# Expert weights in 1 MB loads with 8 KB rows instead of 512 KB loads with 4 KB rows

## The chip, the cores and the metric

The kernel runs on one core of a Trainium2 chip. The metric is the device time of one execution in microseconds (us); the median of three runs counts. TensorE (PE) multiplies matrices; its weight loads (PEld) overlap its products. VectorE (DVE), ScalarE (ACT) and GpSimd (POOL) work element by element, and SyncE (SP) does little more than issue DMA transfers. A core has 16 DMA engines, which share all transfers. "Share" of DMA is the mean busy share of these 16, and can pass 1 a little, since packets overlap in the records.

## The reference

Two transformer-like blocks run one after the other on 256 tokens of width 1024, all in fp32. The first mixes a convolution with a window attention and then sends each token to 2 of 32 experts. The second mixes a long convolution with an attention over the tokens and 256 context rows, and then runs a PEER layer: for each token and each of 8 heads, 16 of 16,384 small experts are looked up by product keys. Cut to what the change touches:

```python
def run_block(args):                       # MoE: 32 experts, D = 1024, F = 512
    tok, wt, e = args
    xb = xt[tok]
    hmid = jax.nn.silu(xb @ w_gate[e]) * (xb @ w_up[e])
    return (hmid @ w_down[e]) * wt[:, None]

def chunk(xc):                             # PEER: 8 heads, 2 x 128 keys
    q = (xc @ wq).reshape(PEER_CHUNK, PEER_HEADS, 2, half)
    s1 = jnp.einsum('chd,hnd->chn', q[:, :, 0], keys1)
    s2 = jnp.einsum('chd,hnd->chn', q[:, :, 1], keys2)
    ...                                    # top 16 of 16 x 16 sums: experts eidx, gates g
    a = jnp.einsum('chkd,cd->chk', u_tab[eidx], xc)
    return jnp.einsum('chk,chkd->cd', gelu(a) * g, v_tab[eidx])
```

An expert's gate and up matrices are 1024 x 512, its down matrix 512 x 1024: 2 MB each, 6 MB in all, and 192 MB for 32 experts.

## The kernel before, in words

All weights are streamed from HBM once, and nearly all go through one helper, `wload` (L67 to L88). It takes the next buffer of a ring (`self.wpools`, walked by the counter `wi`) and has SP issue one transfer of 512 KB into it: 128 partitions, 4 KB in each. A buffer is a pool's tile, so its transfer waits until the last reader of what stood in it is done. SP issues its transfers in the order of its own instruction list: one that waits for a buffer holds up those behind it.

The ring changes with the stage. `wA` has 4 buffers throughout. The first mix (0 to 204 us) has `wA` and 7 buffers of `wB`; the expert stage (204 to 694 us) has 4 `wA`, 7 `wB` and 3 `wC`, 14 buffers or 7 MB, and before them takes 16 places that are free just once (`self.early`: tiles of `l2`, `wE` and the split buffers `hi` and `lo`), so that experts' weights arrive during the first mix. The second mix (694 to 920 us) has 4 `wA` and 3 `wD`; its last part and the query product have `wA` alone; PEER has `wA`, `hi`, `lo` and four parts of a tile named `xm`.

In the expert stage TensorE follows the order in which the program is written (L846 to L893; the order is pinned). For expert e: `expert_up` (L1023, the product in L1031) takes four pairs of a gate and an up load; for each of its 8 slices of 128 rows it runs one gate and one up product side by side in the two halves of the array's columns, 16 products in 8 pairs, each product of 512 columns being listed by the profile in more than one piece. Then `expert_down` (L1050, the product in L1060) of expert e-1 takes four loads of the down matrix, each for two products. Then come a slice of background work of the second block, the transposes and SiLU of expert e (L1042 to L1047), and for every second expert the return of the results to the tokens (`combine`, L1078). Ahead of expert 28 stands a branch on the chip (L924) for experts with more than 64 tokens, which these inputs don't take; 8 loads of expert 28 are issued ahead of it.

In the mixes and in the query product a weight is split for exact fp32 into `hi` (ACT, L97) and `lo` (DVE, L98); its buffer is free when both are done. The query product has 16 columns of `wq`, one load each, and two loads of the keys (`keysT`, L1574), each of which serves 8 columns and holds a `wA` buffer for so long.

Of the kernel before, what the change touches and what calls it, by code (L numbers as in the profile page):

```python
# [44 lines left out]
class K:  # L45
# [20 lines left out]

    def wload(self, src, shape, eng=None):  # L67
        pools = self.wpools
        p, tag = pools[self.wi % len(pools)]
        self.wi += 1  # L70
        if p is None:

            v = tag[:, :math.prod(shape)]
            if len(shape) == 2:
                v = v.rearrange("p (a b) -> p a b", a=shape[0])
            (eng or self.nc.sync).dma_start(v, src)
            return v
        if self.wrap and self.wi == len(pools):
            self.wpools, self.wrap, self.wi = self.wrap, None, 0
        t = self.T(p, [128, 1024], F32, tag)  # L80
        n = 1
        for s in shape:
            n *= s
# [96 lines left out]
    def build(self):  # L180
        tc, nc, A = self.tc, self.nc, self.A
        with ExitStack() as es:
            keep = es.enter_context(tc.tile_pool(name="keep", bufs=1))
            self.keep = keep
            self.wA = es.enter_context(tc.tile_pool(name="wA", bufs=4))
            self.hp = es.enter_context(tc.tile_pool(name="hp", bufs=3))
# [11 lines left out]
            with ExitStack() as e1:  # L198
                self.l1 = l1 = pool(e1, "l1")
                self.l2 = pool(e1, "l2")  # L200
                ew = ExitStack()
                wB = pool(ew, "wB", 7)
                self.wpools = [(self.wA, "wA")] * 4 + [(wB, "wB")] * 7
                self.h = self.T(l1, [128, 2, D], F32, "h")
# [25 lines left out]
                with ExitStack() as e2:  # L230
                    self.me = pool(e2, "me")
                    self.wE = ExitStack()

                    r = self.wi % len(self.wpools)
                    self.wpools = self.wpools[r:] + self.wpools[:r] + [(pool(e2, "wC", 3), "wC")] * 3
                    self.early = [(self.l2, n) for n in ("kv", "kfc", "kfa0", "kfb0", "kfa1", "kfb1")]
                    self.early += [(pool(self.wE, "wE", 4), "wE")] * 4 + [(self.hp, "hi")] * 3 + [(self.hp, "lo")] * 3
# [501 lines left out]
    def moe(self):  # L739
# [103 lines left out]
        def gu(e):  # L843
            return [lambda kq, w=w: w[e][:, 2 * kq:2 * kq + 2, :] for w in (wg, wu)]

        def experts(lo, hi, pre=None, cur=None):  # L846
# [7 lines left out]
            for e in range(lo, hi + 1):  # L854

                if e < hi:
                    if e % 4 == 0 and e > lo:
                        cur = nxt
                    st = self.expert_up(*gu(e), cur[0][:, :, (e % 4) * 64:(e % 4) * 64 + 64], pre if e == lo else None)
                if e > lo:  # L860
                    y = self.expert_down(mid, lambda j: wd[e - 1][:, j, :], (e - 1) % 2, sws[0],
                                         y if e % 2 == 0 else None)
                if e < hi:
                    back(e)
                    mid = self.expert_mid(st)
                    if pend:
                        self.combine(*pend)
                        pend = None
                    if e % 2 == 0:
                        sws.append(self.selw(cur[1], e % 4))  # L870
                    if e % 4 == 2 and e + 2 < 32:
                        nxt = group(e + 2)
                    back(e, True)
                if e > lo and e % 2 == 0:
                    if pend:
                        self.combine(*pend)
                    pend = y, sws.pop(0)
# [22 lines left out]
        pools = self.wpools  # L900
        self.wi = 0
        self.wpools = pools + self.early
# [5 lines left out]
        pools = self.wpools  # L908
        self.wi = 0
# [3 lines left out]
        self.wpools, self.wi = pools, 8  # L913
        self.gf = self.T(self.hp, [128, D], F32, "hi")
# [5 lines left out]
    def overflow(self, many, wg, wu, wd):  # L920
# [3 lines left out]
        with self.tc.If(many > 64):  # L924
# [12 lines left out]
            for j in range(7):  # L937
# [28 lines left out]

                st = self.expert_up(lambda kq: part(wg, 2 * kq, 2), lambda kq: part(wu, 2 * kq, 2), XT)
                m = self.expert_mid(st)
                sw = self.selw(sw, 0, 1)
                y = self.expert_down(m, lambda i: part(wd, i, 1).rearrange("p k f -> p (k f)"), 0, sw)  # L970
                self.combine(y, sw, 1)
# [47 lines left out]

    def up_load(self, g, u, kq):  # L1020
        return [self.wload(f(kq), [2, 512]) for f in (g, u)]

    def expert_up(self, g, u, XT, pre=None):  # L1023
        nc, me = self.nc, self.me
        p = self.ps()
        for kq in range(4):
            w = pre[kq] if pre else self.up_load(g, u, kq)
            for a in range(2):
                k = 2 * kq + a
                for s in range(2):  # L1030
                    nc.tensor.matmul(p[64 * s:64 * s + 64, :], XT[:, k, :], w[s][:, a, :],  # L1031
                                     start=k == 0, stop=k == 7)
        ex = self.T(me, [128, 512], F32, "ex", 2)
        nc.scalar.activation(ex, p, AF.Copy)
        return ex
# [190 lines left out]
    def mix2(self):  # L1226
# [132 lines left out]
        self.m2e.close()  # L1359
        self.wpools = [(self.wA, "wA")]  # L1360
        self.px = self.rpool("px")
# [180 lines left out]
    def peer(self):  # L1542
# [27 lines left out]
        for m in range(16):  # L1570
            if m > 2:
                next(rg, 0)
            if m % 8 == 0:
                kt = self.wload(A["keysT"][:, m * 128:(m + 8) * 128].rearrange("p (m n) -> p m n", m=8), [8, 128])  # L1574
            if m in first:
# [5 lines left out]
            if late:  # L1581
                score(*late)
            late = (m, q, kt[:, m % 8, :])
            if m == 4:
# [6 lines left out]
        w4 = self.T(self.px, [128, 4, 1024], F32, "xm")  # L1591
        self.wpools = [(self.wA, "wA")] * 4 + [(self.hp, "hi")] * 3 + [(self.hp, "lo")] * 3
        self.wpools += [(None, w4[:, i, :]) for i in range(4)]
        self.wi = 0
        gb = ga = self.pace_pe = None
# [559 lines left out]
```

## Time and profile before

| what | us |
|---|---|
| three runs | 1623.05, 1625.93, 1627.79 |
| median | 1625.93 |
| the profiled execution's own time | 1625.43 |
| its span | 1623.6 |

The span lies 1.8 us below the time of its own execution, and that time 0.5 us below the median. TensorE is busy for 94% of the span, DVE for 59%, ACT for 31%. The core moves 536 MB, 426 MB of them on SP's queue (q1). The mean TensorE clock granted is 0.972 of full speed. Stages are cut by the lines that run: first mix to 204, experts to 694, second mix to 920, query product and routing to 1004, PEER's first table to 1305, gathers to 1404, PEER's second table to the end.

In a timeline row the columns are the start and the duration in us, engine, line, operation, output and input tiles, and in brackets the idle time of the engine ahead of it and what ended it; "issue" means that it waited for nothing that the profile shows. In a list of waits, the engine and line that waited stand left of the arrow and what it waited for right of it, then total us, times, and the longest.

### The profile page before, as it was taken

How to read it: one execution, taken by the hardware profiler on the slowest of the kernel's cores; microseconds unless marked ns; L12 is line 12 of the kernel's file. 1: busy time of each engine (PE TensorE's matmuls, PEld its weight loads, DVE VectorE, ACT ScalarE, POOL GpSimd, SP SyncE). 2: the span in 40 equal slices, each digit the busy share in tenths (PEclk: the TensorE clock that was granted, in tenths of full speed). 3: DMA queues.
4: the chain of work that ended last, by engine and by line, in shares of the span. 5: the costliest groups of instructions: out<-in, count | busy, mean ns of one | idle time of the engine just before them, and what ended most of it. 6: DMA issues, size and time to landing. Idle time of an engine off the chain costs nothing. (4 is left out here: it accounts for less than half of the span.)

```text
span 1623.6 us, 25732 instructions
## 1 busy us (share of the span) xinstructions
PE 1527.8 (94%) x9872; PEld 1200.8 (74%) x9872; DVE 960.9 (59%) x2117; ACT 496.0 (31%) x1222; POOL 120.1 (7%) x122
## 2 busy tenths in 40 slices
PE   7999799999999997979999899999999999699996
PEld 6978644543444443358679699999999999699996
DVE  6986622344535432279888899856667656544443
ACT  4444332232222221155344543235444400000001
POOL 0000000000000000000000100311111112111111
PEclk9999899999999998989999999999999999799998
DMA  9548779999999998965657558999999999999992
GB/s 371 182 132 301 273 277 381 381 418 410 418 419 418 419 418 342 417 223 155 210 185 270 185 169 303 376 404 345 366 363 356 357 409 415 416 413 413 414 414 80
DMA packets 135324, 536.53 MB, mean 330 GB/s; under 512 B 16179, under 2 KB 17180, under 8 KB 122780
## 3 DMA queue, kind: packets, MB, share of 16 engines
q1 hardware_dynamic: 117184, 426.07, 69.1%
q0 software_dynamic: 13824, 100.67, 15.5%
q10 hardware_dynamic: 4188, 8.09, 1.4%
q8 instruction: 79, 1.29, 0.3%
q14 instruction: 49, 0.40, 0.1%
HBM read 532.57 MB, written 2.10 MB: 329 GB/s over the span
## 5 line engine op out<-in xcount | busy, mean ns | idle before, releaser
L1793 DVE SCALAR_TENSOR_TENSOR g<-g,xd 128x1024 f32<-128x1024 f32 x96 | 117.5, 1224 | 140.6 <-DMA g<-in_uv_dram,gi 140.6
L1031 PE MATMUL ps<-wB,XT 128*64 128x512 f32 x492 | 133.2, 609 | 4.7 <-PEq L924 4.6
L1765 POOL DMA_INDIRECT g<-in_uv_dram,gi x96 | 98.8, 1029 | 505.6 <-PE ps L1648 121.1
L132 PE MATMUL ps<-xh,hi 128*128 128x256 f32 x416 | 122.9, 296 | 1.6 <-ACT hi L97 1.6
L1067 DVE SCALAR_TENSOR_TENSOR eyl<-ps,slotw,eyh 64x512 fp32r<-64x512 f32 x64 | 47.6, 743 | 119.0 <-ACT eyh L1066 118.7
L138 PE MATMUL ps<-xh,lo 128*128 128x256 f32 x416 | 117.4, 283 | 0.5 <-DVE lo L98 0.5
L137 PE MATMUL ps<-xl,hi 128*128 128x256 f32 x416 | 117.5, 283 | 0.3 <-DVE xl L305 0.3
L1794 ACT ACTIVATE ga<-ga 128x1 f32<-128x1 f32 x96 | 19.4, 202 | 314.9 <-DVE g L1793 314.9
L1031 PEld LDWEIGHTS ps<-wB,XT 128*64 128x64 f32 x492 | 39.6, 139 | 80.5 <-issue 74.0
L97 ACT ACTIVATE hi<-wA 128x1024 fp32r<-128x1024 f32 x63 | 66.6, 1059 | 76.6 <-PE ps L137 28.8
L98 DVE TENSOR_TENSOR lo<-wA,hi 128x1024 fp32r<-128x1024 f32 x63 | 77.7, 1237 | 20.2 <-ACT hi L97 18.2
L1640 PE MATMUL ps<-x,wA 128*128 128x160 f32 x608 | 87.4, 302 | 0.1
L1648 PE MATMUL ps<-B,wA 128*128 128x160 f32 x608 | 85.9, 300 | 0.0
L1640 PEld LDWEIGHTS ps<-x,wA 128*128 128x128 f32 x608 | 84.9, 193 | 0.3 <-issue 0.3
L132 PEld LDWEIGHTS ps<-xh,hi 128*128 128x128 f32 x416 | 79.3, 191 | 7.7 <-issue 4.4
L1080 DVE TENSOR_TENSOR h<-h,ps 128x512 f32<-128x512 f32 x64 | 42.2, 682 | 70.3 <-PE ps L1078 70.3
L1648 PEld LDWEIGHTS ps<-B,wA 128*128 128x128 f32 x608 | 83.5, 190 | 0.0
L137 PEld LDWEIGHTS ps<-xl,hi 128*128 128x128 f32 x416 | 79.4, 191 | 3.9 <-issue 3.1
L1640 PE MATMUL ps<-x,xm 128*128 128x160 f32 x576 | 81.4, 299 | 0.0
L1648 PE MATMUL ps<-B,xm 128*128 128x160 f32 x576 | 81.2, 302 | 0.0
L1779 DVE SCALAR_TENSOR_TENSOR xd<-g,gw,xd 128x1024 f32<-128x1024 f32 x62 | 79.7, 1285 | 2.1
L1648 PEld LDWEIGHTS ps<-B,xm 128*128 128x128 f32 x576 | 80.1, 193 | 0.0
(531 smaller groups left out, 3364.4 us busy)
## 6 DMA issues: line engine op xcount, KB each, us to landing
wB<-in_w_gate_dram SPq DMA_DIRECT2D x70, 512.0 KB
wB<-in_w_down_dram SPq DMA_DIRECT2D x63, 512.0 KB
wB<-in_w_up_dram SPq DMA_DIRECT2D x53, 512.0 KB
wA<-in_ws_dram SPq DMA_DIRECT2D x51, 512.0 KB
wA<-in_ut_dram SPq DMA_DIRECT2D x38, 512.0 KB
wA<-in_v_dram SPq DMA_DIRECT2D x38, 512.0 KB
wA<-in_w_gate_dram SPq DMA_DIRECT2D x36, 512.0 KB
wA<-in_w_up_dram SPq DMA_DIRECT2D x36, 512.0 KB
```

What stands on the lines that cost most here:

```text
L97: ins = self.nc.scalar.activation(hi, w, AF.Copy)
L98: self.last_split = self.nc.vector.tensor_tensor(lo, w, hi.bitcast(F32), op=OP.subtract)
L132: ins = mm(ps, ah, bh, start=first, stop=False)
L137: mm(ps, ah, bl, start=False, stop=False)
L138: mm(ps, al, bh, start=False, stop=last)
L1031: nc.tensor.matmul(p[64 * s:64 * s + 64, :], XT[:, k, :], w[s][:, a, :], start=k == 0, stop=k == 7)
L1067: nc.vector.scalar_tensor_tensor(y[1][r, s, :], p[r, :], w, y[0][r, s, :].bitcast(F32), op0=OP.mult, op1=OP.subtract)
L1640: self.pace_pe = nc.tensor.matmul(p, w[:, k, :], x32[:, k, N0:], start=k == 0, stop=k == 7)
L1648: self.pace_pe = nc.tensor.matmul(acc[k][:, N0:], w[:, k * 128:(k + 1) * 128], B[:, c, :], start=c == 0, stop=c == 127)
L1765: ins = nc.gpsimd.indirect_dma_start(out=buf[i], out_offset=None, in_=A["uv"], in_offset=bass.IndirectOffsetOnAxis(ap=self.gi[:, i // J, i ...
L1779: stt(acc, t, w, acc, op0=OP.mult, op1=OP.add)
L1793: stt(t, t, 1.0, self.gx[s], op0=OP.mult, op1=OP.mult, accum_out=a)
```

## The change

The rings are rebuilt from tiles that hold two loads (8 KB per partition, 1 MB). A pool's entry now says how many halves a tile has. `wload` still loads 512 KB; where the tile has two halves, the next call fills the second half of the same tile, which is a transfer of its own. A new helper, `wload2`, is used by the experts alone: it fills a whole tile with one transfer of 1 MB, a row of 8 KB in each partition. So `up_load` now fetches half a gate and half an up matrix in two transfers where four stood, and `expert_down` half a down matrix. A tile is free when both its halves have been read.

The rings: first mix 2 `wA` and 3 `wB` of 1 MB (10 halves where there were 11); experts 2 + 3 + 2 (7 MB as before); the places for the early loads are the same, four of them now two tiles of 1 MB; second mix 2 `wA` of two halves and 3 `wD` of one; query product 2 `wA` of two halves. The counter is reset where a ring begins. The two loads of `keysT` become one of 1 MB into a buffer of the gather pool (`g`), which is not in use then. The arithmetic is unchanged.

```diff
-    def wload(self, src, shape, eng=None):
+    def pools(self, *groups):
+        self.wpools = [g[:2] + g[3:] for g in groups for _ in range(g[2])]
+        self.wi, self.half = 0, None
+    def wload(self, src, shape, eng=None):
+        n = math.prod(shape)
+        if self.half is None:
+            p, tag, m = self.wnext()
...
+                t = self.T(p, [128, 1024 * m], F32, tag)
+            if m > 1:
+                self.half = t[:, 1024:]
+        else:
+            t, self.half = self.half, None
...
+    def wload2(self, src, shape):
+        if self.half is None and self.wpools[self.wi % len(self.wpools)][2] > 1:
+            p, tag, m = self.wnext()
+            t = self.T(p, [128, 2048], F32, tag).rearrange("p (i a b) -> p i a b", i=2, a=shape[0])
+            self.nc.sync.dma_start(t.rearrange("p i a b -> p (i a) b"), src(0, 2))
+            return [t[:, i] for i in range(2)]
+        return [self.wload(src(i, 1), shape) for i in range(2)]
...
-            self.wA = es.enter_context(tc.tile_pool(name="wA", bufs=4))
+            self.wA = es.enter_context(tc.tile_pool(name="wA", bufs=2))
...
-                wB = pool(ew, "wB", 7)
-                self.wpools = [(self.wA, "wA")] * 4 + [(wB, "wB")] * 7
+                self.pools((self.wA, "wA", 2, 2), (pool(ew, "wB", 3), "wB", 3, 2))
...
-                    self.wpools = self.wpools[r:] + self.wpools[:r] + [(pool(e2, "wC", 3), "wC")] * 3
+                    self.wpools = self.wpools[r:] + self.wpools[:r] + [(pool(e2, "wC", 2), "wC", 2)] * 2
...
-                    self.wpools = [(self.wA, "wA")] * 4 + [(pool(self.m2e, "wD", 3), "wD")] * 3
+                    self.pools((self.wA, "wA", 2, 2), (pool(self.m2e, "wD", 3), "wD", 3, 1))
...
-        pre = [self.up_load(*gu(28), kq) for kq in range(4)]
-        self.wpools = pools[-3:]
+        pre = [self.up_load(*gu(28), kk) for kk in range(2)]
+        self.wpools = pools[-2:]
...
-    def up_load(self, g, u, kq):
-        return [self.wload(f(kq), [2, 512]) for f in (g, u)]
+    def up_load(self, g, u, kk):
+        return [self.wload2(lambda i, n: f(2 * kk + i, n), [2, 512]) for f in (g, u)]
...
-        for kq in range(4):
-            w = pre[kq] if pre else self.up_load(g, u, kq)
-            for a in range(2):
-                k = 2 * kq + a
+        for kk in range(2):
+            w = pre[kk] if pre else self.up_load(g, u, kk)
+            for a in range(4):
+                k = 4 * kk + a
...
+        w2 = [self.wload2(lambda i, n: d(2 * jj + i, n), [1, 1024]) for jj in range(2)]
         for j in range(4):
-            w = self.wload(d(j), [1024])
+            w = w2[j // 2][j % 2][:, 0, :]
...
-        self.wpools = [(self.wA, "wA")]
+        self.pools((self.wA, "wA", 1, 2))
...
-            if m % 8 == 0:
-                kt = self.wload(A["keysT"][:, m * 128:(m + 8) * 128].rearrange("p (m n) -> p m n", m=8), [8, 128])
+            if m == 0:
+                kt = self.T(self.gp, [128, 2 * D], F32, "g").rearrange("p (m n) -> p m n", m=16)
+                nc.sync.dma_start(kt, A["keysT"].rearrange("p (m n) -> p m n", m=16))
```

TensorE, DVE and GpSimd keep their instructions and, but for a few neighbours that change places, their order. What moves is SP's list. First the loads of one expert in the middle of the expert stage, which SP had before as twelve rows (the tile's name carries its buffer's number, then the tensor read and the shape):

```order
L87 DMA wB_658_3329<-in_w_gate_dram 128x1024
L87 DMA wB_659_3331<-in_w_up_dram 128x1024
L87 DMA wB_660_3337<-in_w_gate_dram 128x1024
L87 DMA wB_661_3339<-in_w_up_dram 128x1024
L87 DMA wA_662_3345<-in_w_gate_dram 128x1024
L87 DMA wA_663_3347<-in_w_up_dram 128x1024
L87 DMA wA_664_3353<-in_w_gate_dram 128x1024
L87 DMA wA_665_3355<-in_w_up_dram 128x1024
L87 DMA wB_668_3364<-in_w_down_dram 128x1024
L87 DMA wB_669_3368<-in_w_down_dram 128x1024
L87 DMA wB_670_3372<-in_w_down_dram 128x1024
L87 DMA wC_671_3376<-in_w_down_dram 128x1024
```

Now SP has six rows for one expert in that place, each twice as large:

```order
L104 DMA wC_598_3277<-in_w_gate_dram 128x2048
L104 DMA wA_599_3279<-in_w_up_dram 128x2048
L104 DMA wB_600_3289<-in_w_gate_dram 128x2048
L104 DMA wB_601_3291<-in_w_up_dram 128x2048
L104 DMA wB_604_3304<-in_w_down_dram 128x2048
L104 DMA wA_605_3306<-in_w_down_dram 128x2048
```

The sequence of matrices is the same; what moved is that the two loads of one matrix are now one, so a gate half comes whole before its up half. The second place is SP's list at the end of the second mix and the start of the query product, before (`ws2` holds weights of the second mix, `x2d` is a copy of the activations to HBM):

```order
L87 DMA wA_1865_8829<-in_ws2_dram 128x1024
L87 DMA wA_1868_8847<-in_ws2_dram 128x1024
L87 DMA wA_1871_8853<-in_ws2_dram 128x1024
L87 DMA wA_1890_8962<-in_wq_dram 128x1024
L87 DMA wA_1893_8968<-in_wq_dram 128x1024
L87 DMA wA_1899_9025<-in_keysT_dram 128x1024
L87 DMA wA_1903_9035<-in_wq_dram 128x1024
L87 DMA wA_1913_9086<-in_wq_dram 128x1024
L87 DMA wA_1919_9133<-in_wq_dram 128x1024
L1540 DMA x2d_1887_8944<-x2_1837_8718 128x2x1024
```

And SP's list there now, where x2 behind a row is two transfers into the halves of one tile:

```order
L96 DMA wA_1564_8247<-in_ws2_dram 128x1024 x2
L1595 DMA g_1613_8511<-in_keysT_dram 128x2048
L96 DMA wA_1579_8300<-in_ws2_dram 128x1024 x2
L96 DMA wA_1584_8335<-in_ws2_dram 128x1024 x2
L96 DMA wA_1605_8449<-in_wq_dram 128x1024 x2
L96 DMA wA_1617_8521<-in_wq_dram 128x1024 x2
L96 DMA wA_1632_8618<-in_wq_dram 128x1024 x2
L1560 DMA x2d_1602_8431<-x2_1556_8209 128x2x1024
```

The keys moved ahead of the last four `ws2` loads and out of the `wA` ring, and six columns of `wq` rather than five stand ahead of the copy `x2d`.

## Rows read from the trace of the kernel before

**Rows 1.** The page's slices (40.6 us each): TensorE busy, GB/s moved.
```profile
PE   7999799999999997979999899999999999699996
GB/s 371 182 132 301 273 277 381 381 418 410 418 419 418 419 418 342 417 223 155 210 185 270 185 169 303 376 404 345 366 363 356 357 409 415 416 413 413 414 414 80
```

**Rows 2.** Busy us by window: window, length, PE, PEld, DVE, ACT, POOL, clock, DMA share, GB/s.
```profile
320.00:600.00 280.00, 277.95 (x1287) 117.52 (x1287) 120.69 (x215) 71.52 (x126) 0.00 (x0) 1.00 1.03 417
...
632.00:644.00 12.00, 7.51 (x22) 2.53 (x24) 2.49 (x6) 0.00 (x0) 0.00 (x0) 0.57 0.52 178
644.00:692.00 48.00, 45.00 (x196) 16.43 (x194) 11.44 (x21) 7.60 (x14) 0.00 (x0) 1.00 1.01 407
...
250.00:290.00 40.00, 40.00 (x198) 17.02 (x196) 12.16 (x23) 10.52 (x20) 0.00 (x0) 1.00 1.02 415
...
694.00:920.00 226.00, 209.03 (x1419) 175.24 (x1418) 191.21 (x336) 109.47 (x195) 6.86 (x6) 0.96 0.65 212
920.00:1004.00 84.00, 78.19 (x630) 76.53 (x629) 81.10 (x399) 38.04 (x75) 4.07 (x3) 0.99 0.62 216
```

**Rows 3.** TensorE's weight loads in the expert stage (timeline).
```profile
294.05 0.21 PEld L1060 LDWEIGHTS ps<-wA,em 128*64 128x64 f32 x4 [2.28 <-DMA wA<-in_w_down_dram]
...
321.76 0.20 PEld L1031 LDWEIGHTS ps<-wA,XT 128*64 128x64 f32 x4 [0.36 <-PE ps L1078]
322.25 0.14 PEld L1031 LDWEIGHTS ps<-wA,XT 128*64 128x64 f32 x2 [0.28 <-issue]
322.68 0.14 PEld L1031 LDWEIGHTS ps<-wA,XT 128*64 128x64 f32 x2 [0.29 <-issue]
...
591.55 0.20 PEld L1031 LDWEIGHTS ps<-wC,XT 128*64 128x64 f32 x4 [0.37 <-issue]
...
685.59 0.20 PEld L1060 LDWEIGHTS ps<-wB,em 128*64 128x64 f32 x4 [1.03 <-DMA wB<-in_w_down_dram]
```

**Rows 4.** Waits of TensorE's weight loads for down matrices, 280 to 600.
```profile
PEld ps L1060 <- DMA wA<-in_w_down_dram: 11.6, 11, 2.3
PEld ps L1060 <- DMA wC<-in_w_down_dram: 2.7, 3, 1.0
...
PEld ps L1060 <- DMA wB<-in_w_down_dram: 1.3, 3, 0.6
```

**Rows 5.** SP's waits for buffers that TensorE reads, 300 to 330, then 425 to 460.
```profile
SPq L87 <- PE ps L1031: 11.0, 5, 6.1
...
SPq L87 <- PE ps L1031: 9.6, 7, 2.8
```

**Rows 6.** DMA by queue, 10 to 18: packets, MB, share of 16 engines.
```profile
q1 hardware_dynamic: 691, 2.54, 77.4%
q10 hardware_dynamic: 124, 0.82, 24.2%
```

**Rows 7.** DMA by queue, 1320 to 1560.
```profile
DMA packets 20869, 99.39 MB, mean 414 GB/s; under 512 B 2322, under 2 KB 2322, under 8 KB 15177
...
q1 hardware_dynamic: 14457, 52.66, 54.8%
q0 software_dynamic: 6396, 46.50, 46.9%
```

**Rows 8.** Clock after a wait of TensorE for weights (columns of rows 2).
```profile
294.00:298.00 4.00, 3.94 (x15) 2.34 (x16) 0.76 (x1) 1.19 (x2) 0.00 (x0) 0.57 1.04 310
```

**Rows 9.** The chain of waits in the query product: start, us, what.
```profile
944.31 5.58 DMA wA<-in_wq_dram
950.04 0.92 issue
```

**Rows 10.** DVE's longest waits, 900 to 966.
```profile
DVE lo L98 <- ACT hi L97: 3.4, 4, 1.2
```

**Rows 11.** ACT's waits for weights in the second mix, 700 to 920, then TensorE's for ACT.
```profile
ACT hi L97 <- DMA wA<-in_ws_dram: 15.3, 8, 5.0
...
PE ps L132 <- ACT hi L97: 0.7, 1, 0.7
```

More of the change, by code (lines that the diff above doesn't have):

```diff
@@ L64, in ps, with wnext @@
         return self.T(self.pp, [128, 512], dt, "ps")
-    def wload(self, src, shape, eng=None):
+    def pools(self, *groups):
+        self.wpools = [g[:2] + g[3:] for g in groups for _ in range(g[2])]
+        self.wi, self.half = 0, None
+    def wnext(self):
         pools = self.wpools
-        p, tag = pools[self.wi % len(pools)]
+        e = pools[self.wi % len(pools)]
         self.wi += 1
[L71 to L77, printed above, removed]
         if self.wrap and self.wi == len(pools):
             self.wpools, self.wrap, self.wi = self.wrap, None, 0
[L80 to L83, printed above, removed]
+        return e
+    def wload(self, src, shape, eng=None):
+        n = math.prod(shape)
+        if self.half is None:
+            p, tag, m = self.wnext()
+            if p is None:
+                t = tag
+            else:
+                t = self.T(p, [128, 1024 * m], F32, tag)
+            if m > 1:
+                self.half = t[:, 1024:]
+        else:
+            t, self.half = self.half, None
         v = t[:, :n]
@@ L234, in build @@
                     r = self.wi % len(self.wpools)
-                    self.wpools = self.wpools[r:] + self.wpools[:r] + [(pool(e2, "wC", 3), "wC")] * 3
-                    self.early = [(self.l2, n) for n in ("kv", "kfc", "kfa0", "kfb0", "kfa1", "kfb1")]
-                    self.early += [(pool(self.wE, "wE", 4), "wE")] * 4 + [(self.hp, "hi")] * 3 + [(self.hp, "lo")] * 3
+                    self.wpools = self.wpools[r:] + self.wpools[:r] + [(pool(e2, "wC", 2), "wC", 2)] * 2
+                    self.half = None
+                    self.early = [(self.l2, n, 1) for n in ("kv", "kfc", "kfa0", "kfb0", "kfa1", "kfb1")]
+                    self.early += [(pool(self.wE, "wE", 2), "wE", 2)] * 2
+                    self.early += [(self.hp, "hi", 1)] * 3 + [(self.hp, "lo", 1)] * 3
                     def late():
@@ L843, in gu @@
         def gu(e):
-            return [lambda kq, w=w: w[e][:, 2 * kq:2 * kq + 2, :] for w in (wg, wu)]
+            return [lambda q, n, w=w: w[e][:, 2 * q:2 * (q + n), :] for w in (wg, wu)]
         def experts(lo, hi, pre=None, cur=None):
@@ L900, in moe @@
         pools = self.wpools
-        self.wi = 0
+        self.wi, self.half = 0, None
         self.wpools = pools + self.early
@@ L908, in moe @@
         pools = self.wpools
-        self.wi = 0
-        pre = [self.up_load(*gu(28), kq) for kq in range(4)]
-        self.wpools = pools[-3:]
+        self.wi, self.half = 0, None
+        pre = [self.up_load(*gu(28), kk) for kk in range(2)]
+        self.wpools = pools[-2:]
         self.overflow(many, wg, wu, wd)
-        self.wpools, self.wi = pools, 8
+        self.wpools, self.wi, self.half = pools, 4, None
         self.gf = self.T(self.hp, [128, D], F32, "hi")
@@ L965, in part @@
                     return w[bass.ds(e, 1), :, a:a + n, :].rearrange("a p k f -> p (a k) f")
[L967 removed]
+                st = self.expert_up(lambda q, n: part(wg, 2 * q, 2 * n), lambda q, n: part(wu, 2 * q, 2 * n), XT)
                 m = self.expert_mid(st)
                 sw = self.selw(sw, 0, 1)
[L970 removed]
+                y = self.expert_down(m, lambda j, n: part(wd, j, n), 0, sw)
                 self.combine(y, sw, 1)
@@ L1582, in peer @@
                 score(*late)
-            late = (m, q, kt[:, m % 8, :])
+            late = (m, q, kt[:, m, :])
             if m == 4:
@@ L1591, in peer @@
         w4 = self.T(self.px, [128, 4, 1024], F32, "xm")
-        self.wpools = [(self.wA, "wA")] * 4 + [(self.hp, "hi")] * 3 + [(self.hp, "lo")] * 3
-        self.wpools += [(None, w4[:, i, :]) for i in range(4)]
-        self.wi = 0
+        self.pools((self.wA, "wA", 2, 2), (self.hp, "hi", 3, 1), (self.hp, "lo", 3, 1))
+        self.wpools += [(None, w4[:, i, :], 1) for i in range(4)]
         gb = ga = self.pace_pe = None
```

4 lines of the change are left out of this document (2 added, 2 removed).

## The prediction

> **What bounds the kernel now.** I read the page's slices first, then busy time by window, then TensorE's and SP's waits in the expert stage. In the slices the reader sees two kinds of stretch: DMA stands near 418 GB/s from the seventh slice to the seventeenth, the experts, and again in the last third, while between them TensorE is full and DMA half idle [rows 1]. The change makes transfers larger only where the experts' weights are read, so that stage decides. From 320 to 600 us both sides are nearly full: DMA moves 417 GB/s, and TensorE is busy for 277.95 of 280 us at full clock [rows 2]. An expert is 6 MB (6.29 million bytes), 15.09 us at 417 GB/s. TensorE starts the up products of one expert at 321.76 and those of the expert 18 further on at 591.55 [rows 3], 14.99 us each. So TensorE runs at the pace of the transfers, and the ring lends it a little.
>
> How far is TensorE's own pace from that? From 280 to 600 its weight loads waited for down matrices 17 times, 15.6 us in all [rows 4]. Of each wait 0.29 us is the ordinary gap between two pairs [rows 3], 4.9 us together, so 10.7 us are true waits. That is the most that faster transfers can return in these 320 us. In other places it is SP that waits: 11.0 us between 300 and 330 and 9.6 us between 425 and 460 for buffers that TensorE still reads [rows 5]. There the ring is full, and a lead that the transfers have won is given up.
>
> **The price of a byte.** Two windows hold both kinds of row. Between 10 and 18 us queue q10 brings the attention's bias table, whose rows are 8 KB in a partition: 0.82 MB in 24.2% of 128 engine-us, 26.5 KB per us and engine; q1, with 4 KB rows, brings 2.54 MB in 77.4%, 25.6 [rows 6]: 8 KB rows are 3.3% cheaper. Between 1320 and 1560 the gathers on q0 read rows of 8 KB, 46.50 MB in 46.9% of 3840, 25.8; q1 25.0 [rows 7]: 3.2%. But that mixture moves 414 GB/s in all [rows 7], not more than 4 KB rows alone with 417. So the gain lies between 0 and 3.3%. I take 2.5%, near the two direct readings, with something off for packets that overlap already (a share of 1.03 [rows 2]).
>
> Here the Trainium skill says less: by "DMA: Bandwidth & Descriptors", section "Why small descriptors are slow (HBM only)", each packet costs about three cycles beside its 32-byte beats. That would be 131 cycles for 4 KB and 259 for 8 KB, a gain of 1.2%, my estimate from that page. The rows read 3.2 and 3.3%, and the measurement decides. By the rule the rate terms below would be about half as large and the forecast 1625.9.
>
> **What the rate returns.** The lead grows from the last moment when the ring was full to the waits that follow. There are three such stretches before the branch: 250 to 294, where the long waits end [rows 3] and the transfers ran at 415 GB/s [rows 2]; 320 to 420, after SP's stand [rows 5]; and the last 48 us before 600. That is 44 + 100 + 48 us; 2.5% is 1.1 + 2.5 + 1.2 = 4.8 us, well inside the 10.7. Bounds: 0, and 10.7.
>
> **What the larger pieces take.** Two neighbouring pairs of an up product start 0.43 us apart (322.25 and 322.68 [rows 3]). Before, four such slots free a gate and an up load, 1 MB every 1.7 us, and two slots a down load, 0.5 MB every 0.86. Now eight slots free 2 MB, every 3.4 us, and four free 1 MB. Two things follow. Where the ring is full, the next transfer starts up to 1.7 us later. And where TensorE waits for the last piece of a matrix, it has four slots left to do when it comes, not two: 0.86 us more. The waits lie in four clusters (around 294, 357, 410 and 600, nearly all of the 17 [rows 4]), so the price is 4 x 0.86 = 3.4 to 4 x 2.57 = 10.3 us; nothing excludes zero, if the queue of transfers already issued covers the later start and the wait shrinks as much. I take 3.5: between issue and landing there is a queue that covers most late starts, but nothing covers the last piece.
>
> **The end of the stage.** Ahead of the branch 4 MB are issued, as before, and DMA falls to 178 GB/s and the clock to 0.57 from 632 to 644 [rows 2]; that is unchanged. The four experts behind it are bound by transfers again, 407 GB/s from 644 to 692 [rows 2], with a wait for a down matrix until 685.59, the last of them [rows 3]. 46 us at 2.5% are 1.15 us less; the larger last piece gives 0.86 back: -0.3. Bounds -1.5 and +0.9.
>
> **The query product.** DVE is busy for 81.1 of 84 us from 920 to 1004 [rows 2]; the chain of waits goes through a `wq` load, 5.58 us and then 0.92 [rows 9], and DVE waited 3.4 us for ACT's split [rows 10]. Before, the keys hold one of four buffers, so three are left for sixteen columns; now all four serve them, in two pairs. I take a saving of 1.5 us of the 3.4. Bounds: -3.4, all of it, and +1, if a pair freed late costs more than the fourth buffer brings. The new buffer of the keys comes from memory that the attention left long before, and no other queue is passed.
>
> **The second mix and the rest.** The keys' 1 MB now stands ahead of the last four `ws2` loads: 1.05 MB at 417 GB/s, 2.5 us. And `wA` frees two halves at once. What hides this is slack: ACT waited 15.3 us in 8 waits for these weights, and TensorE waited 0.7 us for ACT's split [rows 11]. I take +0.5; bounds -1 and +5, the latter when the 2.5 us come through twice, once at the keys and once at a pair. The first mix has 10 halves for 11 and PEER four of 14 buffers in pairs: 0, within 1 us either way; where that cover fails, a load is late by 1.25 us (512 KB at 417 GB/s). SP issues some 270 transfers fewer: 0, since it waits in this stage anyway [rows 5].
>
> **The sum.** -4.8 + 3.5 - 0.3 - 1.5 + 0.5 = -2.6 us. The profiled execution took 1625.43 us, 0.5 below the median of 1625.93, so the forecast is 1622.8.
>
> **The rivals.** *First: the rate decides, and TensorE follows.* If rows of 8 KB give 3.3% and the ring's price vanishes in the queue, the true waits of 10.7 us go, the last four experts give 1.5, and the query product up to 3.4: 12 to 15 us, and with some of it kept by TensorE's own work 1611 to 1617, 1614 in the middle. For it speak two direct readings [rows 6, 7], against it SP's stands [rows 5], which show that TensorE, not DMA, is the bound for part of the stage. The Trainium skill leans this way: "DMA: Bandwidth & Descriptors", section "Rules for kernel authors", asks for at least 1 MiB per DMA. Loads of 512 KB reach 417 GB/s here, with others queued behind them, so the size of a load by itself can promise little.
>
> *Second: the pieces decide, and the time grows.* If a larger row gains nothing in a stream that is already full (414 against 417 GB/s [rows 7]), the ring's price stays alone: +3.5, +0.9 at the last expert, and a new wait among the first experts, where the ring has just turned from small early places to large tiles. A wait of 2.28 us before 294 was followed by a clock of 0.57 for 4 us [rows 3, 8], which costs 1.7. With -1.5 and +0.5 as above: +5.1, 1630.5; with the upper price of the pieces, 1637. It decides from where 238 us (the 192 and the 46) gain less than the 3.4 us that are left (3.5 + 0.9 - 1.5 + 0.5), a rate gain of 1.4%, or 2.1% if the clock falls too. Against it speaks that a queue of issued transfers stands ahead of most waits.
>
> *Third: the pairs hold up the second mix.* Each of the 8 waits of ACT [rows 11] grows by the 1.25 us of a second half, 10 us, of which the slack covers a part: +5 to +10 over the rest of the sum, 1628 to 1633. Against it: TensorE hardly waits for ACT there.
>
> **How the numbers follow.** A difference of 0.3%, 4.9 us, is about what a measurement of this kernel can tell from no change; the limits are 1621.0 and 1630.8. The likeliest case has a chance of 0.50, with a range of its own of 1618 to 1628; of it 0.14 lies below 1621.0 and 0.36 between the limits. The first rival has 0.22, all faster. The second has 0.20, 0.15 of it slower. The third has 0.08, 0.06 slower. Faster 0.36, the same 0.43, slower 0.21. The range from 1611 to 1634 takes in the first rival and the lower half of the second.
>
> **What would show it.** In the profile after: the rate from 320 to 600 (427 GB/s by 2.5%; 417 says that the row's length is nothing); the start of the up products 18 experts apart (14.99 now; 14.6 would be the first rival); TensorE's waits for down matrices (fewer clusters, each longer); a drop of the clock among the first experts (second rival); the piece of 5.58 us gone from the chain; TensorE's waits for ACT in the second mix above 3 us (third). The forecast is wrong if the expert stage alone moves by more than 5 us, or if the second mix or PEER moves by more than 3.

## The result, and the profile after

The changed kernel took 1633.71 us (median of 7 runs, 1630.06 to 1635.52), the kernel before, on the same chip, 1623.22 (7 runs, 1621.46 to 1628.14). The ratio is 1.0053, with an interval of [1.0035, 1.0072]: slower, by 10.5 us by the medians, where 2.6 us less were forecast. The time lies inside the predicted range, but the sign is wrong. The profiled execution took 1635.52 us, with a span of 1633.7.

The page's slices after, TensorE busy and GB/s (40.8 us each), to be laid beside [rows 1]:

```profile
PE   7999799999999998879998898999999999699996
GB/s 368 148 140 306 290 275 379 370 425 415 411 420 421 406 413 355 423 187 151 220 185 241 219 156 272 334 413 381 352 366 354 362 400 415 415 413 413 415 413 93
```

The expert stage has one slice of 425 and others of 406 to 421, so the rate is not simply higher. Busy time by window (window, length, PE, PEld, DVE, ACT, POOL, clock, DMA share, GB/s) splits this:

```profile
320.00:600.00 280.00, 278.64 (x1280) 119.14 (x1278) 120.62 (x215) 70.84 (x125) 0.00 (x0) 1.00 1.00 416
330.00:365.00 35.00, 34.80 (x159) 14.31 (x156) 13.75 (x31) 12.30 (x18) 0.00 (x0) 1.00 1.01 426
646.00:694.00 48.00, 42.74 (x194) 16.57 (x191) 10.93 (x21) 7.27 (x13) 0.00 (x0) 1.00 1.00 411
884.00:930.00 46.00, 34.79 (x175) 28.69 (x175) 35.31 (x64) 19.18 (x29) 1.11 (x2) 0.89 0.61 219
```

Where the stream never stops, from 330 to 365, DMA moves 426 GB/s. The kernel before moved 418 there, and 417 in the whole stage [rows 2]:

```profile
330.00:365.00 35.00, 34.71 (x178) 16.01 (x176) 17.14 (x39) 14.97 (x24) 0.00 (x0) 1.00 1.03 418
```

Yet the mean from 320 to 600 is 416. The DMA share there is 1.00 after 1.03 [rows 2]: transfers are cheaper, and the engines stand idle in places. SP's waits for buffers that TensorE reads say why (300 to 330, then 425 to 460, as in [rows 5]):

```profile
SPq L104 <- PE ps L1050: 22.6, 3, 14.3
...
SPq L104 <- PE ps L1050: 24.9, 4, 11.6
```

These were 11.0 and 9.6 us. In the kernel before, SP also waited 7.6 and 15.2 us there for transfers to land; after, no such wait is listed. So in these stretches the ring is full, and TensorE alone sets the pace. TensorE's own waits for weights from 280 to 600, to be laid beside [rows 4]:

```profile
PEld ps L1080 <- DMA wB<-in_w_down_dram: 3.6, 4, 1.7
PEld ps L1050 <- DMA wA<-in_w_up_dram: 3.3, 3, 1.3
PEld ps L1050 <- DMA wB<-in_w_up_dram: 2.6, 1, 2.6
PEld ps L1050 <- DMA wC<-in_w_up_dram: 1.1, 2, 1.0
PEld ps L1080 <- DMA wC<-in_w_down_dram: 0.8, 2, 0.5
PEld ps L1080 <- DMA wA<-in_w_down_dram: 0.5, 1, 0.5
```

They are 13 waits and 11.9 us. Before there were 17 waits and 15.6 us for down matrices [rows 4] and 7 more, of 2.2 us in all, ahead of up products. More than half now falls on up matrices, since a gate half comes whole before its up half. TensorE's timeline, whose first two rows are the starts of the up products 18 experts apart as in [rows 3], the third the first product behind the branch, the last one a transpose early in the second mix:

```profile
324.15 0.13 PEld L1050 LDWEIGHTS ps<-wB,XT 128*64 128x64 f32 x1 [0.36 <-PE ps L1098]
595.66 0.13 PEld L1050 LDWEIGHTS ps<-wC,XT 128*64 128x64 f32 x1 [0.37 <-issue]
639.50 0.18 PEld L1050 LDWEIGHTS ps<-wA,XT 128*64 128x64 f32 x1 [4.54 <-issue]
707.71 0.29 PEld L298 LDWEIGHTS ps<-ident,xxr 128*128 128x128 f32 x2 [6.25 <-issue]
```

(595.66 - 324.15) / 18 is 15.08 us an expert, after 14.99. The transpose stood at 705.66 before: 2.05 us late at the end of the expert stage, so it is not here that the 10 us went. One profile is not exact to this: in three further kernels with the same first 700 us (below) the transpose lies at 704.27, 706.83 and 706.95, and in three with the stage of before at 704.59, 705.09 and 705.41. By the means, 706.4 and 705.2, the change costs about 1.2 us up to there. Some 0.7 us of it stand already at the first up product (at 208.4 us in the mean of these four, at 207.7 in the four with the stage of before), so in the expert stage itself it is about 0.6.

The 10 us went at one place in the second mix. TensorE's last weight load ahead of the output product starts at 891.86 after 891.19, only 0.67 us behind the kernel before. The first one of the output product itself comes 9.28 us late, at 900.59 (below) after this row of the kernel before:

```profile
891.31 0.19 PEld L132 LDWEIGHTS ps<-hi,xh 128*128 128x128 f32 x1
```

Another 12 us on, TensorE is 11.2 us behind (914.50 after 903.30). The place is the last part of the second mix, its output product, where the only weights buffers left are `wA`. SP's timeline before (the last eight `ws2` loads, here `in_ws_dram`, go out one by one as buffers come free):

```profile
879.25 0.33 SPq L87 DMA_DIRECT2D wA<-in_adat_dram  x1
882.19 19.16 SPq L87 DMA_DIRECT2D wA<-in_ws_dram  x8
902.60 0.33 SPq L87 DMA_DIRECT2D wA<-in_wq_dram  x1
```

and after:

```profile
879.35 0.33 SPq L96 DMA_DIRECT2D wA<-in_ws_dram  x1
879.73 0.43 SPq L96 DMA_DIRECT2D wA<-in_adat_dram  x1
882.30 0.33 SPq L96 DMA_DIRECT2D wA<-in_ws_dram  x1
882.68 0.42 SPq L96 DMA_DIRECT2D wA<-in_adat_dram  x1
895.80 3.30 SPq L96 DMA_DIRECT2D wA<-in_ws_dram  x4
899.20 0.38 SPq L1595 DMA_DIRECT2D g<-in_keysT_dram  x1
```

Between 882.68 and 895.80 SP issues nothing. Both `wA` tiles hold a `ws2` load in the first half and, in the second, one of the last two loads of `adat`, a 512 KB slice each, 32 of them, which `ada2()` takes for the modulation that is needed later. DVE reads those in between other work, and the last two late, at 894.52 and 897.00; three rows of the kernel after, DVE's timeline with the first of these two reads, SP's wait from 880 to 910, and TensorE's timeline at the first weight load of the output product:

```profile
894.52 1.22 DVE L453 SCALAR_TENSOR_TENSOR wA<-wA,scb 128x1024 f32<-128x1024 f32 x1
```

```profile
SPq L96 <- DVE wA L453: 16.3, 3, 12.7
```

```profile
900.59 0.29 PEld L150 LDWEIGHTS ps<-hi,xh 128*128 128x128 f32 x1 [8.54 <-ACT hi L115]
```

The first of the two tiles is not free until its second half has been read at 895.7. SP stands for 12.7 us, the first `ws2` load after it lands late, ACT's split is late, and TensorE stands for 8.54 us where before it went on at 891.31. Before, two of the four `wA` buffers held an `adat` slice as late, and the other two carried the stream; DVE's reads in the kernel before:

```profile
894.34 1.22 DVE L434 SCALAR_TENSOR_TENSOR wA<-wA,scb 128x1024 f32<-128x1024 f32 x1
898.62 1.22 DVE L434 SCALAR_TENSOR_TENSOR wA<-wA,scb 128x1024 f32<-128x1024 f32 x1
```

The clock granted from 884 to 930 fell to 0.89 (window above); in the kernel before it was 0.96 in this window.

### The profile page after: what moved, and what is told of

Read it like the earlier page. It is cut to its first block, busy times and chain, and to the rows that moved or that the text cites. A ratio compares the mean times of both kernels' runs of the same rounds, so it can differ in the third digit from the quotient of the medians.

```text
span 1633.7 us, 25258 instructions
## 1 busy us (share of the span) xinstructions
PE 1529.5 (94%) x9872; PEld 1208.5 (74%) x9872; DVE 960.8 (59%) x2117; ACT 493.8 (30%) x1220; POOL 119.7 (7%) x122
## 3 DMA queue, kind: packets, MB, share of 16 engines
q1 hardware_dynamic: 90256, 426.06, 66.7%
## 5 line engine op out<-in xcount | busy, mean ns | idle before, releaser
L1050 PE MATMUL ps<-wA,XT 128*64 128x512 f32 x280 | 129.3, 604 | 4.5 <-DVEq L943 3.8
L1050 PE MATMUL ps<-wC,XT 128*64 128x512 f32 x272 | 95.3, 596 | 2.7 <-DMA wC<-in_w_up_dram 2.7
```

## The experiments

Theory: sharing a tile between a weight of the output product and an `adat` slice costs the 10 us, and the rest of the change is near zero. Rival one: the larger pieces or the halves in the expert stage cost it. Rival two: the keys, moved ahead of the last `ws2` loads, do. All were run in five rounds beside the kernel before; "ratio" is to that one.

**The `adat` slices alone in a ring of their own** (in the kernel after; the slices take the `wD` buffers, and the second mix's other weights have, from there on, the two `wA` pairs alone):

```diff
-            w = self.wload(self.A["adat"][s], [1024])
+            w = self.T(self.wD, [128, 1024], F32, "wD")
+            nc.sync.dma_start(w, self.A["adat"][s])
...
+        self.pools((self.wA, "wA", 1, 2))
         self.ada_row()
```

> The changed kernel, but in the second mix the modulation loads (adat) get the three wD buffers to themselves, and the weights (ws, ws2) the two wA tiles of two halves to themselves. Theory A (a wA tile holds an adat half that DVE reads late, at 894.5 and 897.0 us, and so the first weights of the output product are issued at 895.8 instead of 882.2): SP's wait of 12.7 us on DVE goes, TensorE's wait of 8.5 us at 900.6 goes, and the time falls by 8 to 10 us, to 1624 to 1626. Rival B (it is the freeing of halves in pairs, whatever they hold): SP still waits for pairs of splits, less than 3 us come back, 1631 to 1634. Rival C (the 1 MB of the keys ahead of the last four ws2 loads): 2.5 us at most come back here, since the keys stand where they stood.

1623.97 us (1621.08 to 1628.55), ratio 1.0006 [0.9995, 1.0017]. Of the 10.5 us, 9.7 are gone, as the theory had it. SP's timeline in this kernel, and the first weight load of the output product on TensorE:

```profile
878.77 0.33 SPq L454 DMA_DIRECT2D wD<-in_adat_dram  x1
881.70 14.19 SPq L96 DMA_DIRECT2D wA<-in_ws_dram  x6
```

```profile
886.96 0.19 PEld L150 LDWEIGHTS ps<-hi,xh 128*128 128x128 f32 x1
```

The stand of 12.7 us is gone, and the product begins at 886.96 without a wait. The experts' loads are those of the kernel after, so rival one falls as the cause of the 10 us.

**Only the last two of the 32 slices moved**, to show that those two are the cause and not the sharing in general:

```diff
-            w = self.wload(self.A["adat"][s], [1024])
+            if s < 30:
+                w = self.wload(self.A["adat"][s], [1024])
+            else:
+                w = self.T(self.wD, [128, 1024], F32, "wD")
+                nc.sync.dma_start(w, self.A["adat"][s])
```

> The changed kernel with one edit: the last two of the 32 modulation loads go to wD instead of into the second halves of the last two wA tiles, so the output product's first weights find wA tiles without such a half. Theory A (these two halves alone, read by DVE at 894.5 and 897.0, hold up the eight ws2 loads): as good as giving all 32 a ring of their own, 8 to 10 us below the changed kernel, 1623 to 1626. Rival B (sharing tiles all through the second mix costs): less than 4 us come back, 1630 or more.

1626.41 us (1621.51 to 1628.15), ratio 1.0014 [0.9998, 1.0029]: two loads of 512 KB account for 7.3 of the 10.5 us, a little less than the 8 to 10 expected and far from rival B. SP's timeline:

```profile
881.72 3.75 SPq L96 DMA_DIRECT2D wA<-in_ws_dram  x4
886.10 1.80 SPq L457 DMA_DIRECT2D wD<-in_adat_dram  x2
891.54 12.64 SPq L96 DMA_DIRECT2D wA<-in_ws_dram  x6
```

A stand of 3.6 us is left (887.9 to 891.5). That the remaining 2.4 us are this one, I did not show.

**Each 1 MB tile filled by two transfers of 512 KB** (4 KB rows, same buffers), in the kernel after and in the kernel with the `adat` ring:

```diff
-            self.nc.sync.dma_start(t.rearrange("p i a b -> p (i a) b"), src(0, 2))
+            for i in range(2):
+                self.nc.sync.dma_start(t[:, i], src(i, 1))
```

> The changed kernel, but each 1 MB tile of the experts is filled by two loads of 512 KB with 4 KB rows: the ring as coarse as in the changed kernel, the rows as short as before. If the 8 KB rows bring the 4.8 us of the forecast in the expert stage, this one is later at the branch by 3.5 to 5 us than the changed kernel and takes 1636 to 1639. If TensorE, not the rate, sets the end of the stage, it is within 1.5 us of the changed kernel, 1632 to 1635, with 417 GB/s where that has 428.

> The kernel with the modulation loads in their own ring (1623.97), but each 1 MB tile of the experts filled by two loads of 512 KB with 4 KB rows. If the longer rows are worth the 4.2 us that separated the two kernels with the shared tiles (1637.87 against 1633.71): 1627 to 1629. If that difference was mostly the second mix, and TensorE sets the pace of the experts: 1624 to 1626, with the branch reached 0.5 to 2 us later.

In the kernel after: 1637.87 us (1636.88 to 1640.96), 1.0088 [1.0073, 1.0104], 4.2 us above it by the medians. With the `adat` ring: 1626.41 (1621.87 to 1630.11), 1.0017 [1.0004, 1.0030], 2.4 above. Windows from 330 to 365, and SP's queue in them (packets, MB, share of 16 engines): first the kernel with the `adat` ring and 8 KB rows, then the same with 4 KB rows:

```profile
330.00:365.00 35.00, 34.88 (x164) 14.98 (x161) 14.53 (x33) 13.08 (x19) 0.00 (x0) 1.00 1.01 426
...
q1 hardware_dynamic: 2041, 14.88, 101.0%
```

```profile
330.00:365.00 35.00, 34.65 (x165) 14.47 (x162) 14.84 (x33) 13.38 (x20) 0.00 (x0) 1.00 1.03 417
...
q1 hardware_dynamic: 4000, 14.58, 102.4%
```

Row and size of the load are all that differs: 426 against 417 GB/s, 2.2% more. In the time of their packets the engines move 3.5% more (14.88 MB in 101.0%, 14.58 in 102.4%); the rate gains less, since the packets overlap less (a share of 1.01 after 1.03). Over the whole stage, 320 to 600, the gain is smaller still: 416 to 419 GB/s in the four kernels with 8 KB rows, 414 in both with 4 KB. And the transpose at the start of the second mix, at 706.4 us in the mean of the four kernels with 8 KB rows, lies at 707.32 and 707.29 in these two: 0.9 us later, and 2.1 later than in the four with the stage of before. So the new buffers by themselves cost about 2.1 us up to there (1.5 of them behind the first up product), and the rows give 0.9 of it back, both small beside the spread of 3.4 us among the four. The first time lies where a gain of 4.8 us from the rows was expected, but not for that reason: this kernel comes to the branch at 638.49, 1.0 us ahead of the kernel after, and falls behind it only in the second mix, where the two are the same. The second comes there 2.7 us later than its partner (639.27 after 636.61), and its time lies between the two expected ranges. The medians say 2.4 and 4.2; the intervals of the pair with the `adat` ring overlap. The rows' gain lies between 1 and 4 us, not settled closer.

**The keys alone** (the kernel before with both halves of `keysT` in one load into `g`):

```diff
-            if m % 8 == 0:
-                kt = self.wload(...)
+            if m == 0:
+                kt = self.T(self.gp, [128, 2 * D], F32, "g")...
```

> The kernel before, with the two loads of the keys made one of 1 MB into a buffer of the gather pool, and nothing else. The forecast's term for the query product: -1.5 us (bounds -3.4 and +1), 1620 to 1624, the piece of 5.58 us on a wq load gone from the chain. Rival C: the 1 MB ahead of the last weights of the second mix delays them by up to 2.5 us, so that it is 1 to 2.5 us slower than before.

1623.97 us (1621.65 to 1627.03), 1.0001 [0.9991, 1.0011]: nothing. Rival two falls; but my saving of 1.5 us isn't there either. In its profile this kernel is 1.3 us ahead at 910 us and at 1000 us 2.4 on TensorE and 3.0 on DVE, so the saving is made in the query product. Then TensorE stands, at a weight load for two transposes of the routing (timeline):

```profile
1008.40 0.29 PEld L1926 LDWEIGHTS ps<-ident,x 128*128 128x128 f32 x2 [6.42 <-DVE x L1919]
```

In the kernel before, these two (the second row below) wait for nothing; it waits 2.11 us at the transpose ahead of them and 2.68 at those of the routing's second half, where the kernel with the keys moved has no wait:

```profile
1003.70 0.14 PEld L1925 LDWEIGHTS ps<-ident,x 128*128 128x128 f32 x1 [2.11 <-issue]
1011.99 0.28 PEld L1925 LDWEIGHTS ps<-ident,x 128*128 128x128 f32 x2
...
1051.98 0.29 PEld L1925 LDWEIGHTS ps<-ident,x 128*128 128x128 f32 x2 [2.68 <-DVE x L1918]
```

With the keys moved, the two transposes stand 20 products earlier in TensorE's list, ahead of what DVE has to finish for them. So TensorE's order did change by more than a few neighbours here, unlike what the section on the change says. The kernel after has the same wait, at 1019.87, of 6.39 us.

**The transposes six steps later**, to see what such a wait is worth: an `if t == 0: for _ in range(6): yield` ahead of them makes the scheduler place other products first. In the kernel with the `adat` ring, in the kernel before, and in the kernel before with the keys moved:

```diff
+            if t == 0:
+                for _ in range(6):
+                    yield
             p = self.ps()
             for i in range(3):
                 nc.tensor.transpose(...)
```

> The kernel with the modulation loads in their own ring (1623.97), and the three transposes of the first half of the routing written six steps later, so that on TensorE they stand three and a half groups of eight products (2.2 us each) further behind. Theory E (what the keys' own buffer gains in the query product is given back where TensorE's queue stands 6.4 us on those transposes): the 6.4 us wait goes, 3 to 5 us less, 1619 to 1621. Rival F (the wait only moves, to the later transposes or to the gathers, which then start later): 1623 to 1626.

> The kernel before, with nothing but the routing's first transposes written six steps later. If the gain of the version at 1618.11 is the order of TensorE alone, this one has it too: 4 to 6 us below before, 1618 to 1620. Theory E (the later transposes only let through what the keys' own buffer gains): TensorE waits only 2.1 and 2.7 us there in the kernel before, so at most 2 us less, 1622 to 1624.

> The kernel before, with the keys in the gather pool's buffer and the transposes six steps later; loads of 512 KB as before. Theory E: the query product's gain comes through, 2 to 4 us below before, 1620 to 1622. What then is left to 1618.11 (2 to 4 us) is the share of the experts' loads of 1 MB and of the rings of the second mix. If it is at 1618 itself, the 1 MB loads bring nothing; if at 1624, the keys bring nothing.

| kernel | us | ratio |
|---|---|---|
| `adat` ring, later transposes | 1618.11 (1611.57 to 1622.10) | 0.9969 [0.9952, 0.9986] |
| before, later transposes | 1615.53 (1612.13 to 1619.82) | 0.9946 [0.9932, 0.9961] |
| before, keys in `g`, later transposes | 1618.42 (1611.68 to 1622.04) | 0.9965 [0.9950, 0.9980] |

The second beats both kernels by more than either expectation: 4 to 6 us if the order alone counts, 2 at most by theory E, and it is 9.4 by the medians. Windows around the routing, the kernel before and then that one:

```profile
996.00:1060.00 64.00, 59.69 (x414) 59.22 (x414) 52.29 (x169) 14.40 (x48) 12.59 (x8) 0.95 0.88 323
```

```profile
996.00:1060.00 64.00, 63.82 (x471) 63.55 (x471) 52.08 (x167) 11.48 (x43) 11.94 (x10) 1.00 0.91 348
```

and its two places of the transposes on TensorE, for which the kernel before waited 2.11 and 2.68 us:

```profile
1008.78 0.20 PEld L1928 LDWEIGHTS ps<-ident,x 128*128 128x128 f32 x2 [0.45 <-DVE x L1918]
...
1056.74 0.39 PEld L1928 LDWEIGHTS ps<-ident,x 128*128 128x128 f32 x3
```

TensorE is busy for 4.1 us more of 64, and the granted clock is 1.00 instead of 0.95, which is 3.2 us of 64: 7.3 of the 9.4 us by the medians. Where the other 2 are is not shown. Two waits of 4.8 us together, in a stretch that TensorE bounds, thus cost half as much again as their length by this window, and almost twice by the medians. The keys in `g` show no gain even without the wait at the transposes: a new one takes its place, TensorE for ACT from 1010 to 1025 (3.4 us in the kernel with the `adat` ring):

```profile
PEld ps L1641 <- ACT B L1602: 2.5, 1, 2.5
```

**The expert loads alone** (1 MB tiles in `wB`, in the first mix too, and in `wC`; four single buffers in `wA`, the keys and all else as before). The edit, here and in the next cut, is against the kernel after:

```diff
-            self.wA = es.enter_context(tc.tile_pool(name="wA", bufs=2))
+            self.wA = es.enter_context(tc.tile_pool(name="wA", bufs=4))
...
-                self.pools((self.wA, "wA", 2, 2), (pool(ew, "wB", 3), "wB", 3, 2))
+                self.pools((self.wA, "wA", 4, 1), (pool(ew, "wB", 3), "wB", 3, 2))
```

> The kernel before in all but the pools wB and wC, which have 1 MB tiles (three and two), filled by loads of 1 MB with 8 KB rows in the expert stage; wA keeps its four buffers of 512 KB, the second mix, the query product, the keys and PEER are as before. Theory A (the loss is all in the second mix; in the expert stage rate and coarser pieces cancel): 0 to +2 us against before, 1623 to 1625.5, start of the branch within 3 us of before. Rival D (the expert stage's coarser ring loses, and what follows only moves with it): +4 us or more, 1627 and up.

1634.14 us (1627.78 to 1635.03), 1.0052 [1.0034, 1.0070]. By the time alone rival one would have won, but the trace shows another cause, a fault of this edit. TensorE's waits from 180 to 215:

```profile
PE ps L777 <- DMA wC<-in_wr_dram: 5.0, 1, 5.0
```

The matrix of the router, `wr`, fell behind ten more early loads of the experts than before (19 stand ahead of it, 9 before), and TensorE was some 6 us late before the stage began. Within the stage it lost 0.8 us more. So the run didn't test its question, and I gave `wr` its place back:

```diff
-                    self.half = None
+                    self.wi, self.half = 0, None
```

> As e2_moe_only (1 MB tiles in wB and wC alone, all else as in the kernel before), but the ring's counter starts anew with the expert stage, so that the router's weights (wr) stand ahead of the early expert loads and not behind ten of them. Theory A: the 6 us that the kernel without this lost at 186 us were the router's wait for wr (5.0 us); with it gone the experts' 1 MB loads alone are worth between -2 and +2 us: 1622 to 1627. Rival D (the coarser ring of the experts loses by itself): 1628 and up.

1629.26 us (1621.60 to 1633.17), 1.0037 [1.0021, 1.0052], above the 1622 to 1627 of theory A and in the range of rival D, a coarser ring that loses by itself. But the expert stage goes from 0.6 us ahead at its start to 0.4 behind at its end; the larger loss stands again at the transposes, here those of the routing's second half (TensorE's waits, 996 to 1070):

```profile
PEld ps L1947 <- DVE x L1940: 6.5, 2, 5.5
```

So I ran it once more with the transposes six steps later.

> The same with the routing's first transposes six steps later. If the 1 MB loads of the experts bring anything when everything else is as before, this is below the 1615.53 of the kernel before with the later transposes: 1613 to 1615. If rate and ring cancel, 1615 to 1618.

1617.55 us (1611.95 to 1620.29), 0.9960 [0.9946, 0.9975], where it was expected if rate and ring cancel. Its profile, though, loses 4.2 us in the expert stage, against 0.8 and 1.1 in the two others with these tiles, so that stage is not settled closer than this. Of the four kernels with later transposes, none with a part of the change is below the one without any. The intervals overlap, so that a loss isn't shown; a gain isn't either.

## Why the prediction was wrong

**The step that failed** is "The second mix and the rest": "`wA` frees two halves at once. What hides this is slack", taken at +0.5 us with bounds of -1 and +5. TensorE was 2.05 us late at the start of the second mix and 11.2 at its end, so the term measured about +9; at the output product alone it lost 10.5. By the prediction's own sign (the second mix moves by more than 3 us) it is wrong here. The slack was counted from ACT's waits for landing weights [rows 11], summed over a stage that has seven buffers for most of its length. In the last part only the `wA` pairs are left, and there the question is not how late a load may land but who reads the two halves of a tile last: both had an `adat` slice as the second, and SP stood for 12.7 us until DVE had read the first of these two slices. Moving the slices away gives 9.7 us back, moving two of them 7.3. After the change ACT waited 29.8 us for `ws2` weights in `wA` from 700 to 930, 15.3 before. SP's order after the change has the two tensors in turns in the same tiles, just ahead of the rows that I took from it.

**The third rival** named the right stage, and its sign came true: TensorE waited for ACT's split for far more than 3 us (700 to 930; 0.7 us before [rows 11]):

```profile
PE ps L150 <- ACT hi L115: 9.8, 3, 8.3
```

Its time, 1628 to 1633, is close to the measured 1633.71, but by luck: it made it of eight waits longer by 1.25 us each, and it was one stand of SP, of 12.7 us, in one place. Its chance of 0.08 rested on "TensorE hardly waits for ACT there", true of the kernel before, whose buffers come free one by one.

**The price of a byte** held where the stream never stops: 427 GB/s were forecast at 2.5%, and 426 were measured from 330 to 365, 2.2% over 417. In the window named for it, 320 to 600, it was 416, and by that sign the row's length would have counted for nothing: SP's stands hid the gain. The direct readings of 3.2 and 3.3% [rows 6, 7] are the time of the packets, which measured 3.5%; that the rate gains less, as packets overlap, was rightly allowed for. The rule of the Trainium skill ("DMA: Bandwidth & Descriptors", section "Why small descriptors are slow (HBM only)"), from which I had worked out an estimate of 1.2%, is too low for either figure.

**What the rate returns** was the right mechanism with the wrong size: -4.8 and -0.3 were forecast; the runs that differ in the row and size of the load alone give 1 to 4 us. The term had no place for a full ring. SP's stands for TensorE doubled (22.6 and 24.9 us), and the lead that the transfers won was given up there; [rows 5] had shown it, and I used them only to say where a lead begins.

**What the larger pieces take**: the waits came in fewer pieces, 13 for 24, each a little longer (0.9 us on average after 0.7), and more than half moved to the up matrices, which I didn't foresee. Their price by itself, in the two kernels with the new buffers and 4 KB rows, is about 1.5 us over the expert stage, under half of the +3.5. Rate and pieces together came to about +0.6 us in that stage instead of -1.6: small, as forecast, and beside the scatter of the profiles its sign is not shown. The fall of the clock among the first experts, the sign of the second rival, didn't come: it was 1.00 from 250 to 320.

**The end of the stage** was to have the same dip: from 632 to 646 DMA moved 265 GB/s after 200, at a clock of 0.63 in both, and the first product came at 639.50 after 636.46. The four experts behind it ran at 411 GB/s after 407.

**The query product**: the piece of 5.58 us [rows 9] left the chain of waits, and the lag behind the kernel before fell from 11.2 to 9.3 us across it, close to the -1.5. But the time didn't follow, since TensorE's order put the transposes ahead of their operands: the kernel with the keys alone has a ratio of 1.0001. DVE's wait for ACT [rows 10] even grew, to 6.8 us in 5 waits. I costed the edit where it happens and not where its lead is next used.

**Smaller readings** that move no term: SP issues 187 transfers fewer, not some 270 (q1 has 90,256 packets after 117,184, and a transfer is 144 of them, 128 rows and 16 small ones). The four clusters hold 13 of the 17 waits for down matrices. DMA stands near 418 GB/s from the ninth slice, not the seventh [rows 1].

## What to carry to other kernels

When two loads share a buffer, look up the last reader of each half before anything else: the buffer is free when the slower of them is done, and a small side load in the second half can hold up a stream that has no other buffer. Where the ring is full, a faster transfer is worth only what TensorE still waits for. And a saving ahead of an engine whose list is in order must be followed to the next instruction that depends on another engine: if that one waits, the saving is given back there.

## What the runs showed that I had not expected

Removing two waits of TensorE, 2.11 and 2.68 us, by order alone gained 9.4 us by the medians and made the best kernel of all, 1615.53 us. The clock granted from 996 to 1060 rose from 0.95 to 1.00 with them gone. With a wait of 6.4 us in that window (the keys alone, and the `adat` ring) it was 0.92.

What stays open is why parts of the change still cost 2 to 3 us beside that kernel once the transposes are later (1617.55, 1618.11 and 1618.42 against 1615.53, intervals overlapping). Their profiles name a place in each: in the two with the keys in `g`, TensorE waits 2.5 and 3.4 us for ACT at a clock of 0.97 and 0.95 from 996 to 1060; in the one with the experts' loads alone the clock is 1.00 there, and the expert stage loses 4.2 us.
